# Output projection of a hybrid encoder layer: operands split inside the last branch block, first weights requested one block earlier, merged tiles fetched in eight steps

## The chip, the cores and the metric

The kernel runs on one core of a Trainium2 chip. The core has a matrix engine (TensorE, PE in the profile; PEld is its weight load), a vector engine (VectorE, DVE), a scalar engine (ScalarE, ACT), a general engine (GpSimd, POOL) and an engine that issues most DMA transfers (SyncE, SP). Each works through its own instructions in the order in which they stand; they wait for each other by semaphores. The metric is the time of one execution in device microseconds (us).

## The reference, cut to what matters

One encoder layer on x of 1024 rows and 2048 columns, in float32. The part that the change touches is the end:

```
y_a = windowed_gqa(q, k, v, ...) * silu(gate_a)
y_p = multiscale_pool(u, ...) * silu(gate_p)
g_a, g_p = split(sigmoid(h @ w_merge + b_merge))
merged = g_a * (y_a @ w_br_attn) + g_p * (y_p @ w_br_pool)
o = merged @ w_out                                    # 1024x2048 by 2048x2048
x + gate * rmsnorm(o, post_g)
```

So there are two branch products (1024 by 1024 by 2048 each), a gated sum called merged, one output product, and a norm over whole rows, which needs the squares of all 2048 columns of a row before any of that row can be written.

## The kernel before

**Numbers.** A float32 product is made of three matmuls: each operand is split into a high part in TensorE's fast float32 form (`hi`, a copy on ScalarE) and the rest (`lo`, a subtraction on VectorE); the product is hi by hi, lo by hi and hi by lo. `split` (line 94) makes the pair; its lines 95 (ScalarE) and 96 (VectorE) stand in the profile for every split.

**Fewer products.** Every large product is cut into two by two blocks and made by the Strassen-Winograd scheme: seven block products, not eight. `MOVING` names the seven moving operands in their order: B11, T3, T2, B21, T4, T1, B22; the weights that go with them are A11, S3, S2, A12, A22, S1, S4. The results build up in PSUM banks called X, V and Z, of two each, and are read out by VectorE and ScalarE; a bank can be written again only after it was read.

**Branch products.** `strassen` (line 210) does 256 output columns of a weight; the loop over `b` and `i` calls it eight times for each branch. `run` (line 321) steps through it; the last of the seven products of one call (B22, held in `late`) is run inside the next call, or by `flush`. Between the products `finish` (line 1065) multiplies a result by its gate and, for the second branch, adds the first branch's part, which comes from DRAM (`mp_d`). The gate is read from DRAM into a ring of four `gt` buffers, `fetch_gate`, and a new one is asked for when an old one has been used; ScalarE makes the sigmoid (line 1057). Merged columns 0 to 511 of the sequence stay in SBUF, in tiles `m` (`mt`, eight of them, two block rows by four `jp`); columns 512 to 1023 go to DRAM (`m_d`) through `pv`, for the second half. `merged_sums` makes the first sums (T1's and T2's operands) of one `jp`.

**Output product.** It is done in four blocks by `out_pair` (line 1163): halves 0 and 1 of the rows, and within each `i` = 0 and 1, two groups of columns. Here the merged values stand on TensorE as the weights, and the output weights are the moving side: in the profile `whi` and `wlo` are the split output weights, `mh` and `ml` the split merged operands. `put_op` (line 1098) makes operand n of one `jp`; both its splits and sums are pinned. One `out_pair` runs the seven products; each asks for four weight tiles (`wr`, 512 KB each, a ring of four), splits them into a ring of four `whi` and four `wlo`, and issues six matmuls for each of eight split weights (lines 1131 to 1133). After each quarter of a product a function is called that does what has to go between: `between_00` makes the next operand and, near its end, loads the other half's merged tiles from `m_d` (16 transfers of 256 KB); `between_01` makes sums and operands of the other half; `between_10` and `between_11` bring back rows of the first half (`mo` from `o_d`, and rows of x), finish them and store them. `pg` are the two rows of gains of a block. In the fourth block the last product's weights are all split ahead, the third block of rows is finished (`third_block`), and then the last two row tiles one by one.

**What sets the order.** A planner in the kernel framework orders the instructions of each engine by its estimates of when they can run, except those that `keep` pins to the program's order. The order is fixed when the kernel is built. TensorE, VectorE, ScalarE and SP then run their lists strictly in that order; a DMA that waits for a buffer or for an earlier store holds up every later DMA on SP.

Of the kernel before, what the change touches and what calls it, by code (L numbers as in the profile page):

```python
# [20 lines left out]
P = 128  # L21
# [21 lines left out]
def encoder_layer(ctx: ExitStack, tc: tile.TileContext, x, c, table, w_ada, b_ada, pre_g,  # L43
# [21 lines left out]
    def pool(name, bufs=1, **kw):  # L65
        return tc.tile_pool(name=name, bufs=bufs, reuse_waits="tile", **kw)
# [9 lines left out]
    def uid(s):  # L76
        cnt[0] += 1
        return f"{s}_{cnt[0]}"
# [4 lines left out]
    def slot(name, dt=F32R, shape=(P, 512)):  # L83
        return big.tile(list(shape), dt, tag="big", name=uid(name))
# [5 lines left out]
    def keep(ins):  # L90

        tc.keep_in_program_order(ins)
# [228 lines left out]
    def run(gen, side=None, every=(0, 2, 4, 6), at=()):  # L321
        for i in range(7):
            if i == 2:
                flush()
            else:
                next(gen)
                if fills:
                    fills.popleft()()
            for n, step in at:
                if n == i:  # L330
                    step()
            if side and i in every:
                side.popleft()()
        late.append(gen)
# [685 lines left out]
    ev_ctx.close()  # L1020
    ev_ctx = ExitStack()
    ev = ev_ctx.enter_context(pool("ev3", 6, side="right"))
    for b, w in enumerate((w_ba, w_bp)):
        op = new_op()
        fill_op(op, range(4), *ys[b], now=7 if b else 3)
        if b == 0:
            side.extend(y_steps(yp_d, ys[1]))
        else:
            ysrc.close()
            ev_ctx.close()  # L1030
            ev_ctx = ExitStack()
            ev = ctx.enter_context(pool("ev4", 4, side="right"))
            mr = ctx.enter_context(pool("mraw", side="right"))

            def merged_tiles():

                return [[mr.tile([P, 2, 512], F32, tag="m", name=uid("m"), bufs=2 * JP) for _ in range(JP)]
                        for _ in range(2)]

            def merged_sums(m, t2, jp):  # L1040

                b12 = m[0][jp][:, :, 256:512]
                keep(sub(b12, b12, m[0][jp][:, :, 0:256]))
                t2[jp] = mr.tile([P, 2, 256], F32, tag="t2", name=uid("t2"), bufs=JP)
                keep(sub(t2[jp], m[1][jp][:, :, 256:512], b12))

            mt, mt2 = merged_tiles(), {}
            side.extend([lambda: None] * 25)
            for jp in range(JP - 1):
                side[6 * jp + 7] = lambda jp=jp: merged_sums(mt, mt2, jp)  # L1050
        gates = {}

        def fetch_gate(i, blk, b=b):
            gt = ev.tile([P, 512], F32, tag="gt", name=uid("gt"), bufs=4)
            load(gt, block(proj_d, NIN + b * D + i * 256)(blk))
            col = 64 + b * KT + 2 * i + (1 if blk[0] == "2" else 0)
            nc.scalar.activation(gt, gt, AF.Sigmoid, bias=cols[:, col:col + 1])  # L1057
            gates[i, blk] = gt

        wanted = deque((i, blk) for i in range(8) for blk in ("11", "21", "22", "12"))  # L1060
        for _ in range(4):
            fetch_gate(*wanted.popleft())

        for i in range(8):
            def finish(blk, ps, addend, res, gates=gates, i=i, b=b):
                gt = gates.pop((i, blk))
                if ps is not None and addend is None:
                    nc.vector.tensor_tensor(res, ps, gt, ALU.mult)
                else:
                    if ps is not None:  # L1070
                        add(res, ps, addend)
                    nc.vector.tensor_tensor(res, res, gt, ALU.mult)
                if b == 0:
                    store(block(mp_d, i * 256)(blk), res)
                else:
                    if blk[1] == "1":
                        dst = mt[int(blk[0]) - 1][i // 2][:, i % 2]
                    else:
                        dst = ev.tile([P, 512], F32, tag="pv", name=uid("pv"), bufs=2)
                    load(dst, block(mp_d, i * 256)(blk))  # L1080
                    add(dst, dst, res)
                    if blk[1] == "2":
                        store(block(m_d, i * 256)(blk), dst)
                if wanted:
                    fetch_gate(*wanted.popleft())

            run(strassen(w, i * 256, rows_apart, range(4), op, ev, finish), side,
                () if b == 0 and i == 0 else (0, 2, 4) if b == 0 or i < 7 else (0, 1, 2, 3))
        flush()
        assert not side  # L1090

    merged_sums(mt, mt2, JP - 1)
    ssq = const.tile([P, NB, 4], F32, name="ssq_o")

    def put_op(n, jp, op, m, t2):


        name = MOVING[n]
        b11, b12, b21, b22 = (m[kh][jp][:, :, c * 256:(c + 1) * 256] for kh in range(2) for c in range(2))
        src = {"B11": b11, "T3": b11, "T2": t2[jp], "B21": b21, "T4": b21, "T1": b12, "B22": b22}[name]
        hi, lo = slot("mh", F32R, (P, 2, 256)), slot("ml", F32R, (P, 2, 256))
        split(hi, lo, src, True)
        op[name][jp] = hi, lo
        if name == "B11":
            keep(sub(b11, t2[jp], b11))
        elif name == "B21":
            keep(sub(b21, b21, t2[jp]))  # L1110

    def fetch_merged(m, kh):
        for jp in range(JP):
            for n in range(2):
                k = 2 * (2 * jp + n) + kh
                load(m[kh][jp][:, n], m_d[k * P:(k + 1) * P, 512:1024])

    def weights(name, i, jp):

# [39 lines left out]
    def row_tiles():  # L1159
        m = mr.tile([P, 2, 512], F32, tag="m", name=uid("mo"), bufs=2 * JP)  # L1160
        return m[:, 0], m[:, 1]

    def out_pair(half, i, op, between, after=None):


# [1 line left out]
        stays = half == 1 or i == 1  # L1167
        count = iter(range(7))
        g = {}
        for nh in range(2):  # L1170
            g[nh] = ev.tile([P, 512], F32, tag="ev", name=uid("pg"))
            n0 = nh * (D // 2) + i * 512
            load(g[nh], pg_d[0:1, n0:n0 + 512].to_broadcast([P, 512]))

        def split_weights(wname, ring=True):
            for jp in range(JP):
                raw = weights(wname, i, jp)
                for jj in range(2):
                    hi, lo = (wp.tile([P, 512], F32R, tag=t, name=uid(t), bufs=4) if ring else slot(t)
                              for t in ("whi", "wlo"))  # L1180
                    split(hi, lo, raw[:, jj])
                    yield hi, lo

        def product(wname, mov, pbs, fresh=False):

            ws = split_weights(wname)
            n, nj = next(count), 2 * JP
            for j in range(nj - 2):
                w = next(ws)
                for t in range(2):  # L1190
                    out_mm(pbs[t], op, mov, j, t, w, fresh and j == 0, False)
                if j % 2:
                    between(n, j // 2)
            w = list(ws)
            for t in range(2):
                for j in (nj - 2, nj - 1):
                    out_mm(pbs[t], op, mov, j, t, w[j - nj + 2], False, j == nj - 1)
            between(n, JP - 1)
# [21 lines left out]
        def kept(tag):  # L1220
# [3 lines left out]
        bx, bz, bv = ([bank(tag, b) for tag in tags] for b, tags in  # L1224
                      (("X", ("mm", "mm")), ("Z", SEEDED), ("V", ("sc", "sc"))))
        product("A11", "B11", bx, True)
        for t in range(2):
            nc.scalar.activation(bz[t], bx[t], AF.Copy)
        product("S3", "T3", bv, True)
# [9 lines left out]
            add(u2[t], bv[t], u2[t])  # L1239
            result("21", t, u2[t], u2[t])  # L1240
        product("S1", "T1", bz)
        ws = list(split_weights("S4", ring=False)) if final else None
        u4 = copies([slot("u4", F32) for _ in range(2)] if final else tiles("u4"), bz)
        for t in range(2):
            add(p7[t], p7[t], u4[t])
            result("22", t, p7[t], p7[t])
# [13 lines left out]
            for n in (0, 2, 3, 1):  # L1260
                finish_block(6 + t, n, scale)

    ops = [new_op(JP), new_op(JP)]
    for jp in range(JP):
        put_op(0, jp, ops[0], mt, mt2)
    nextm, nextt2 = [], {}
    scales = {}
    side = deque()
# [22 lines left out]
    def steps(n):  # L1291
        for _ in range(n):
            if side:
                side.popleft()()

    def between_00(n, jp):
        if n < 6:
            put_op(n + 1, jp, ops[0], mt, mt2)
        if jp == JP - 1 and n == 5:
            nextm.extend(merged_tiles())  # L1300
            fetch_merged(nextm, 0)
        if jp == JP - 1 and n == 6:
            fetch_merged(nextm, 1)

    def between_01(n, jp):

        if n == 1:
            merged_sums(nextm, nextt2, jp)
        for k in ((), (), (0,), (1, 2), (3,), (4,), (5,))[n]:
            put_op(k, jp, ops[1], nextm, nextt2)  # L1310
# [74 lines left out]
```

## Time and profile before

| | |
|---|---|
| median of 3 runs | 2163.8 us (2154.8 to 2165.83) |
| span of the profiled execution | 2152.0 us; the page gives no time around it |
| TensorE busy | 2098.7 us, 98% |
| VectorE, ScalarE busy | 1539.9 us (72%), 1129.6 us (52%) |
| mean granted TensorE clock | 0.996 |
| DMA | 466.11 MB, mean 217 GB/s |

The last branch product ends and the output product begins near 1820 us; the four output blocks take the rest. Times in a timeline are microseconds from the start of the span. A matmul's shown duration overlaps the next one's, so the pace is read from start to start. SPq is SP's queue: a row there is an issue, and the transfer lands some microseconds later.

### The profile page before, as it was taken

The numbers are of one execution on the slowest core, as the hardware profiler recorded it, in microseconds if no ns is written. First come the engines' busy times: TensorE is split into PE (matmuls) and PEld (weight loads), VectorE is DVE, ScalarE is ACT, GpSimd is POOL, SyncE is SP. The second block draws the span as 40 slices with busy tenths as digits, with TensorE's granted clock in tenths as the row PEclk, the third lists the DMA queues.
The fourth block names the chain that finished last, engine by engine and source line by source line (L and its number), as shares of the span: only waits on it lengthen the run. The fifth ranks groups of instructions, "written<-read, shape, count | busy, mean of one in ns | idle before, by whom it ended". The sixth has DMA issues, their size and how long they took to land.

```text
span 2152.0 us, 28951 instructions
## 1 busy us (share of the span) xinstructions
PE 2098.7 (98%) x9567; PEld 1716.3 (80%) x9567; DVE 1539.9 (72%) x2754; ACT 1129.6 (52%) x2124; POOL 7.4 (0%) x66
## 2 busy tenths in 40 slices
PE   6999999999999999999999999999999999999998
PEld 4588888887878888888888887888788887878886
DVE  5786666776547676777776878566967877879666
ACT  5654444443474546767765443334645544757654
POOL 0000000000000000000000000000000000000000
PEclk9999999999999999999999999999999999999999
DMA  9986566898666355545445765755654655686996
GB/s 333 290 277 202 188 203 212 296 316 271 227 224 206 118 175 199 171 158 186 161 150 189 220 223 192 238 177 177 229 175 156 230 167 175 207 287 215 303 314 226
DMA packets 303255, 466.11 MB, mean 217 GB/s; under 512 B 23882, under 2 KB 144866, under 8 KB 303104
## 3 DMA queue, kind: packets, MB, share of 16 engines
q1 hardware_dynamic: 301648, 462.02, 65.3%
q0 software_dynamic: 1120, 2.19, 0.3%
q8 instruction: 75, 1.23, 0.2%
q14 instruction: 76, 0.62, 0.1%
q10 hardware_dynamic: 336, 0.06, 0.0%
HBM read 340.41 MB, written 125.85 MB: 217 GB/s over the span
## 4 chain that ended last, share of the span: by engine, by line
PE 84%; DMA 8%; DVE 4%; ACT 2%; issue 1%; SPq 1%; DVEq 0%; ACTq 0%
PE Z L235 28%; PE X L235 18%; PE V L235 18%; DMA raw<-in_w_merge_dram 3%; PE Z L1131 2%; PE Z L1132 2%; PE Z L1133 2%; PE V L1131 1%; PE V L1133 1%; PE V L1132 1%; PE X L1132 1%; PE X L1133 1%; PE X L1131 1%; DVE wlo L96 1%; DMA xt<-in_x_dram 1%
## 5 line engine op out<-in xcount | busy, mean ns | idle before, releaser
L95 ACT ACTIVATE whi<-raw 128x512 fp32r<-128x512 f32 (+1 forms) x528 | 320.2, 610 | 509.1 <-PE Z L235 265.3
L96 DVE TENSOR_TENSOR wlo<-raw,whi 128x512 fp32r<-128x512 f32 (+1 forms) x528 | 346.9, 662 | 191.4 <-PE Z L235 114.6
L96 DVE TENSOR_TENSOR wlo<-wr,whi 128x512 fp32r<-128x512 f32 x224 | 150.9, 689 | 62.5 <-ACT whi L95 57.7
L95 ACT ACTIVATE whi<-wr 128x512 fp32r<-128x512 f32 x224 | 138.1, 628 | 99.6 <-DVE wlo L96 35.3
L102 DVE TENSOR_TENSOR raw<-raw,raw 128x512 f32<-128x512 f32 x80 | 55.2, 690 | 95.1 <-DMA raw<-in_w_merge_dram 73.2
L235 PE MATMUL V<-T3h,whi 128*128 128x512 f32 x336 | 92.3, 393 | 6.2 <-DVE u L102 6.2
L1057 ACT ACTIVATE gt<-gt,cols 128x512 f32<-128x512 f32 x64 | 46.0, 723 | 99.0 <-DMA gt<-proj_d 74.1
L235 PE MATMUL X<-B11h,whi 128*128 128x512 f32 x336 | 92.5, 393 | 3.2 <-DVE part L102 1.9
L235 PE MATMUL Z<-B22h,whi 128*128 128x512 f32 x336 | 92.8, 395 | 0.9 <-ACT u L290 0.9
L235 PE MATMUL Z<-T1h,whi 128*128 128x512 f32 x336 | 91.8, 392 | 0.9 <-ACT T1h L95 0.9
L235 PE MATMUL V<-T4h,whi 128*128 128x512 f32 x336 | 92.2, 392 | 0.0
L235 PE MATMUL X<-B11l,whi 128*128 128x512 f32 x336 | 92.1, 393 | 0.2 <-DVE B11l L96 0.2
L235 PE MATMUL X<-B11h,wlo 128*128 128x512 f32 x336 | 91.5, 392 | 0.0
L235 PE MATMUL Z<-T2h,whi 128*128 128x512 f32 x336 | 91.3, 391 | 0.0
L235 PE MATMUL Z<-T1l,whi 128*128 128x512 f32 x336 | 91.0, 390 | 0.1
L235 PE MATMUL Z<-B22l,whi 128*128 128x512 f32 x336 | 90.9, 390 | 0.0
L235 PE MATMUL X<-B21h,whi 128*128 128x512 f32 x336 | 90.9, 390 | 0.0
L235 PE MATMUL V<-T3l,whi 128*128 128x512 f32 x336 | 90.9, 390 | 0.0
L235 PE MATMUL V<-T4l,whi 128*128 128x512 f32 x336 | 90.8, 390 | 0.0
L235 PE MATMUL V<-T4h,wlo 128*128 128x512 f32 x336 | 90.8, 389 | 0.0
L235 PE MATMUL Z<-T1h,wlo 128*128 128x512 f32 x336 | 90.7, 390 | 0.0
L235 PE MATMUL Z<-T2l,whi 128*128 128x512 f32 x336 | 90.7, 390 | 0.0
(306 smaller groups left out, 4849.9 us busy)
## 6 DMA issues: line engine op xcount, KB each, us to landing
part<-part_d SPq DMA_DIRECT2D x136, 256.0 KB, 4.9
ada<-in_w_ada_dram SPq DMA_DIRECT2D x128, 256.0 KB, 4.7
raw<-in_w_in_dram SPq DMA_DIRECT2D x64, 512.0 KB, 4.0
raw<-in_w_merge_dram SPq DMA_DIRECT2D x64, 512.0 KB, 5.7
wr<-ws_dS SPq DMA_DIRECT2D x64, 512.0 KB, 5.4
wr<-in_w_out_dram SPq DMA_DIRECT2D x48, 512.0 KB, 5.2
proj_d<-part SPq DMA_DIRECT2D x68, 256.0 KB, 2.2
sw<-in_w_out_dram SPq DMA_DIRECT2D x64, 256.0 KB, 5.4
```

The costliest lines, as they stand in the source:

```text
L95: ins = (nc.scalar.activation(hi, src, AF.Copy), nc.vector.tensor_tensor(lo, src, f32(hi), ALU.subtract))
L96: nc.vector.tensor_tensor(lo, src, f32(hi), ALU.subtract))
L102: return (eng or nc.vector).tensor_tensor(o, a, b, ALU.add)
L235: nc.tensor.matmul(ps, w_[:, i], op[mov][j][m_], start=fresh and i == 0 and n == 0, stop=i == nj - 1 and n == 2, skip_group_check=True)
L1057: nc.scalar.activation(gt, gt, AF.Sigmoid, bias=cols[:, col:col + 1])
L1131: nc.tensor.matmul(pb, hi, w[0], start=first, stop=False, skip_group_check=True)
L1132: nc.tensor.matmul(pb, lo, w[0], start=False, stop=False, skip_group_check=True)
L1133: nc.tensor.matmul(pb, hi, w[1], start=False, stop=last, skip_group_check=True)
```

## The change

1. `put_op` and `ssq` move ahead of the branch loop. In the last call of the second branch (`b == 1 and i == 7`), `run` now does `put_op(0, jp, ...)` for `jp` 0 to 2 after the first, second and third step, and after the sixth step the last `merged_sums` and the last `put_op(0, ...)`. Before, all of these stood after the branch loop.
2. When a block's seventh product begins its last quarter, the four weight tiles of A11 of the next block are requested; `split_weights` uses them later. Before, they were requested when the next block began.
3. The gains `pg` are loaded after a block's first product, not at its start.
4. The second half's merged tiles are fetched in eight pieces of two transfers, over the sixth and seventh product of the first block and the first product of the second. Before: eight transfers after the sixth product and eight after the seventh.
5. In the fourth block six of the eight S4 weights are split, then come the copies of Z (`u4`), then the last two splits, which are pinned.

The amount of work is the same; no instruction is added or removed.

```diff
+            at = []
+            if b == 1 and i == 7:
+                at = [(1 + jp, lambda jp=jp: put_op(0, jp, ops[0], mt, mt2)) for jp in range(JP - 1)]
+                at += [(5, lambda: merged_sums(mt, mt2, JP - 1)), (5, lambda: put_op(0, JP - 1, ops[0], mt, mt2))]
             run(strassen(w, i * 256, rows_apart, range(4), op, ev, finish), side,
-                () if b == 0 and i == 0 else (0, 2, 4) if b == 0 or i < 7 else (0, 1, 2, 3))
+                () if b == 0 and i == 0 else (0, 2, 4) if b == 0 or i < 7 else (0, 1, 2, 3), at)
...
-    merged_sums(mt, mt2, JP - 1)
...
-    def fetch_merged(m, kh):
-        for jp in range(JP):
-            for n in range(2):
-                k = 2 * (2 * jp + n) + kh
-                load(m[kh][jp][:, n], m_d[k * P:(k + 1) * P, 512:1024])
+    def fetch_merged(m, kh, jp):
+        for n in range(2):
+            k = 2 * (2 * jp + n) + kh
+            load(m[kh][jp][:, n], m_d[k * P:(k + 1) * P, 512:1024])
...
+    first_raws = []
...
-        def split_weights(wname, ring=True):
+        def split_weights(wname, ring=True, pin=()):
             for jp in range(JP):
-                raw = weights(wname, i, jp)
+                raw = first_raws.pop(0) if wname == "A11" and first_raws else weights(wname, i, jp)
...
-                    split(hi, lo, raw[:, jj])
+                    split(hi, lo, raw[:, jj], 2 * jp + jj in pin)
...
             w = list(ws)
+            if n == 6:
+                first_raws.extend(weights("A11", 1 - i, jp) for jp in range(JP))
...
         product("A11", "B11", bx, True)
+        fetch_gain()
...
-        ws = list(split_weights("S4", ring=False)) if final else None
+        if final:
+            last = split_weights("S4", ring=False, pin=(6, 7))
+            ws = [next(last) for _ in range(6)]
         u4 = copies([slot("u4", F32) for _ in range(2)] if final else tiles("u4"), bz)
+        if final:
+            ws += list(last)
...
-    for jp in range(JP):
-        put_op(0, jp, ops[0], mt, mt2)
...
+    later = deque((kh, jp) for kh in range(2) for jp in range(JP))
+
+    def fetch_next():
+        if later:
+            fetch_merged(nextm, *later.popleft())
+
     def between_00(n, jp):
         if n < 6:
             put_op(n + 1, jp, ops[0], mt, mt2)
-        if jp == JP - 1 and n == 5:
+        if n == 4 and jp == JP - 1:
             nextm.extend(merged_tiles())
-            fetch_merged(nextm, 0)
-        if jp == JP - 1 and n == 6:
-            fetch_merged(nextm, 1)
+        if n >= 5 and jp:
+            fetch_next()
...
     def between_01(n, jp):
 
+        if n == 0 and jp:
+            fetch_next()
```

More of the change, by code (lines that the diff above doesn't have):

```diff
@@ L1022, in encoder_layer, with put_op @@
     ev = ev_ctx.enter_context(pool("ev3", 6, side="right"))
+    ssq = const.tile([P, NB, 4], F32, name="ssq_o")
+    def put_op(n, jp, op, m, t2):
+        name = MOVING[n]
+        b11, b12, b21, b22 = (m[kh][jp][:, :, c * 256:(c + 1) * 256] for kh in range(2) for c in range(2))
+        src = {"B11": b11, "T3": b11, "T2": t2[jp], "B21": b21, "T4": b21, "T1": b12, "B22": b22}[name]
+        hi, lo = slot("mh", F32R, (P, 2, 256)), slot("ml", F32R, (P, 2, 256))
+        split(hi, lo, src, True)
+        op[name][jp] = hi, lo
+        if name == "B11":
+            keep(sub(b11, t2[jp], b11))
+        elif name == "B21":
+            keep(sub(b21, b21, t2[jp]))
+    ops = [new_op(JP), new_op(JP)]
     for b, w in enumerate((w_ba, w_bp)):
@@ L1085, in finish @@
                     fetch_gate(*wanted.popleft())
+            at = []
+            if b == 1 and i == 7:
+                at = [(1 + jp, lambda jp=jp: put_op(0, jp, ops[0], mt, mt2)) for jp in range(JP - 1)]
+                at += [(5, lambda: merged_sums(mt, mt2, JP - 1)), (5, lambda: put_op(0, JP - 1, ops[0], mt, mt2))]
             run(strassen(w, i * 256, rows_apart, range(4), op, ev, finish), side,
-                () if b == 0 and i == 0 else (0, 2, 4) if b == 0 or i < 7 else (0, 1, 2, 3))
+                () if b == 0 and i == 0 else (0, 2, 4) if b == 0 or i < 7 else (0, 1, 2, 3), at)
         flush()
         assert not side
-    merged_sums(mt, mt2, JP - 1)
[L1096 to L1110, printed above, removed]
-    def fetch_merged(m, kh):
-        for jp in range(JP):
-            for n in range(2):
-                k = 2 * (2 * jp + n) + kh
-                load(m[kh][jp][:, n], m_d[k * P:(k + 1) * P, 512:1024])
+    def fetch_merged(m, kh, jp):
+        for n in range(2):
+            k = 2 * (2 * jp + n) + kh
+            load(m[kh][jp][:, n], m_d[k * P:(k + 1) * P, 512:1024])
     def weights(name, i, jp):
@@ L1169, in out_pair, with fetch_gain @@
         g = {}
[L1170 to L1173, printed above, removed]
-        def split_weights(wname, ring=True):
+        def fetch_gain():
+            for nh in range(2):
+                g[nh] = ev.tile([P, 512], F32, tag="ev", name=uid("pg"))
+                n0 = nh * (D // 2) + i * 512
+                load(g[nh], pg_d[0:1, n0:n0 + 512].to_broadcast([P, 512]))
+        def split_weights(wname, ring=True, pin=()):
             for jp in range(JP):
-                raw = weights(wname, i, jp)
+                raw = first_raws.pop(0) if wname == "A11" and first_raws else weights(wname, i, jp)
                 for jj in range(2):
@@ L1261, in out_pair @@
                 finish_block(6 + t, n, scale)
-    ops = [new_op(JP), new_op(JP)]
-    for jp in range(JP):
-        put_op(0, jp, ops[0], mt, mt2)
     nextm, nextt2 = [], {}
```

## The prediction

> **What bounds the kernel now.** I read the page first, then the list of what TensorE waited for, then the timelines of TensorE, ScalarE, VectorE and the DMA queue around each wait, then the chain of waits. The page gives the span and TensorE's share; the waits are those of the last 652 us, where the output projection (lines 1131 to 1133) lies.
>
> ```profile
> span 2152.0 us, 28951 instructions
> PE 2098.7 (98%) x9567; PEld 1716.3 (80%) x9567; DVE 1539.9 (72%) x2754; ACT 1129.6 (52%) x2124; POOL 7.4 (0%) x66
> PE X L1132 <- DVE ml L96: 3.9, 1, 3.9
> PE X L1131 <- ACT whi L95: 2.9, 1, 2.9
> PE Z L1131 <- ACT u L1206: 2.2, 1, 2.2
> PE V L1131 <- ACT whi L95: 0.8, 1, 0.8
> ```
>
> TensorE is busy 98% of the span, and the change removes no matmul, so it can only win idle time. In the output projection there are four idle places, 9.8 us together. The first has a slow tail (a row of a timeline: start, duration, engine, line, out<-in, idle time before and its releaser):
>
> ```profile
> 1817.56 1.07 PE L235 MATMUL Z<-T1h,whi 128*128 128x512 f32 x4
> 1820.28 0.61 PE L1131 MATMUL X<-whi,mh 128*128 128x512 f32 x2
> 1821.12 1.19 PE L235 MATMUL Z<-B22h,whi 128*128 128x512 f32 x4 [0.23 <-ACT u L290]
> 1828.06 0.80 PE L1132 MATMUL X<-whi,ml 128*128 128x512 f32 x1 [3.92 <-DVE ml L96]
> 1828.65 0.63 PE L1133 MATMUL X<-wlo,mh 128*128 128x512 f32 x1
> 1833.35 0.49 PE L1133 MATMUL X<-wlo,mh 128*128 128x512 f32 x1
> 1833.67 0.39 PE L1131 MATMUL X<-whi,mh 128*128 128x512 f32 x1
> ```
>
> From 1817.56 to 1820.28 twelve matmuls take 2.72, a step of 0.227. From 1820.28 to 1833.67 there are 27 of them (2, then 12 of the last branch product, then 13 singles whose first two and last are shown): 6.1 at that step, 13.4 in fact. **The first place costs 7.3**: some 4.7 of waiting, and after 1828.65 eleven steps of 0.43 (4.70 to 1833.35), that is a slowed clock, for 2.6 with the restart. The others are read below.
>
> **Place 1, operands made in the last branch pair.** `put_op(0, ...)` for three tiles now comes inside the last `strassen`, pinned in program order; TensorE's order hardly changes (two more X matmuls ahead of the last branch product). On VectorE and ScalarE the moved work now stands ahead of things that release others:
>
> ```profile
> 1810.96 0.72 ACT L1057 ACTIVATE gt<-gt,cols 128x512 f32<-128x512 f32 x1 [2.78 <-DMA gt<-proj_d]
> 1813.63 0.62 ACT L95 ACTIVATE mh<-m 128x512 fp32r<-128x512 f32 x1
> 1814.15 0.58 ACT L245 ACTIVATE u<-Z 128x512 f32<-128x512 f32 x1
> 1816.46 0.72 ACT L1057 ACTIVATE gt<-gt,cols 128x512 f32<-128x512 f32 x1 [1.73 <-DMA gt<-proj_d]
> 1812.85 0.68 DVE L1068 TENSOR_TENSOR c<-Z,gt 128x512 f32<-128x512 f32 x1
> 1815.25 0.69 DVE L1068 TENSOR_TENSOR c<-X,gt 128x512 f32<-128x512 f32 x1
> 1818.95 0.68 DVE L102 TENSOR_TENSOR u<-V,u 128x512 f32<-128x512 f32 x1
> 1827.32 0.69 DVE L96 TENSOR_TENSOR ml<-m,mh 128x512 fp32r<-128x512 f32 x1
> 1828.04 0.69 DVE L105 TENSOR_TENSOR m<-t,m 128x512 f32<-128x512 f32 x1
> 1813.56 0.32 SPq L1055 DMA_DIRECT2D gt<-proj_d  x1
> ```
>
> Steps read here: ScalarE 0.52 (0.63 after a gate), VectorE 0.60, or 0.72 where it needs the result just made. In the order that the changed kernel is built with, the first mh starts at 1812.6 (a split and a copy after the gate of 1810.96, ahead of two weight splits), so its ml at 1813.24 and `m<-t,m` at 1813.96 go ahead of `c<-Z,gt`, which moves from 1812.85 to 1814.57. Its end frees the buffer of the last gate: that load moves from 1813.56 to 1815.28, and the sigmoid, which came 2.90 behind the load, from 1816.46 to 1818.18. Behind this sigmoid on ScalarE stand two mh (1818.81, 1819.33) and the first two out weights (to 1820.98). VectorE waits for those mh in order: ml 1819.45, ml, two m differences, and only then `c<-X,gt` at 1821.85, which ran at 1815.25 before. That read frees the bank of the first output tile: TensorE, ready at 1820.28, starts at 1822.56, **2.28** late. Its third matmul waits for wlo (1822.45 to 1823.14): **0.15**. The fourth needs the bank of V, freed by `u<-V,u` at 1823.65 to 1824.34 (1818.95 before): **0.98**. On ScalarE the fourth mh needs the finished tile (`m<-m,c` ends 1823.74); then a weight split; then `u<-Z` at 1824.8 to 1825.4, for which the last branch product waits: **0.84**. It ends at 1828.3, twelve more X matmuls at 1830.9; the next wlo stands thirteen steps of 0.60 behind VectorE's 1824.25, one of them 0.72, at 1832.2 to 1832.9: **2.05**. Together 6.3, with four restarts of 0.11 (from 2132.23 to 2132.57, shown under place 4, is 0.34) 6.7.
>
> Is the clock kept? The lowest price is nothing, the highest the 2.6 just seen. The row nearest to after's idle pieces (2.28 at most, but three within 5 us) is elsewhere in the kernel:
>
> ```profile
> 1330.67 1.19 PE L235 MATMUL X<-B11h,whi 128*128 128x512 f32 x4 [1.85 <-DVE part L102]
> 1331.70 1.83 PE L235 MATMUL X<-B11l,whi 128*128 128x512 f32 x4
> 1333.32 1.91 PE L235 MATMUL X<-B11h,wlo 128*128 128x512 f32 x4
> ```
>
> There 1.85 of idle was followed by two groups of four that took 1.83 and 1.91 instead of 1.07, 1.6 more in all, while the idle 2.93 and 2.20 shown below were followed by none. One in three: I take 0.5. So 7.2 for place 1 after the change against 7.3: **no gain**, between 0.6 gained and 2.0 lost (6.7 to 9.3).
>
> [...]
>
> On SP the first pair's gains (`pg`) now wait for a buffer of the ending branch, with the stores of the last merged rows behind. The second quarter of the second product's weights goes out some 8 us later (about 1833.5); with a landing of 5 to 7 (6.5 and 7.3 below) they come at 1839 to 1841, and are wanted when that product's first quarter is done, about 1842. I cost it at nothing; without that cover it is 2 to 3. No work of POOL's queue is moved or passed.
>
> **Place 2, weights ahead and merged tiles spread (first to second pair).**
>
> ```profile
> 1906.62 0.39 PE L1133 MATMUL Z<-wlo,mh 128*128 128x512 f32 x1
> 1909.93 0.50 PE L1131 MATMUL X<-whi,mh 128*128 128x512 f32 x1 [2.93 <-ACT whi L95]
> 1902.59 6.58 DMA wr<-in_w_out_dram
> 1911.24 0.37 SPq L1122 DMA_DIRECT2D wr<-ws_dS  x1
> DMA to landing us min/median/max: 7.3/7.3/7.3
> 1896.00:1920.00 24.00, 20.96 (x89) 16.11 (x88) 12.93 (x21) 11.69 (x24) 0.00 (x0) 1.00 0.93 303
> ```
>
> The second pair's first A11 weights are issued at 1902.59 and land 6.58 later: TensorE starts 3.31 behind the matmul before, 3.1 lost, some 3.5 with the restarts. The change puts their load ahead of ten transfers of 256 KB (two stores of p, six merged loads, two `pg`); at the 303 GB/s of the last row that is 8.7 of queue, so it is in place and this wait goes. What is late next is the S3 weights: issued at 1911.24, landed 7.3 later at 1918.5. With the wait gone A11 starts at 1906.85, its 48 matmuls take 10.9, and S3 wants its first weights about 0.7 before 1917.7. The transfers ahead are the same (16 merged, 8 stores, 2 `pg`, 12 weights), and the last row (DMA share 0.93) leaves little room to land sooner. With the landing unmoved S3 waits 1.9 with its restart; if the weights' own order closes all gaps, nothing; if `pg` and merged loads pile up, 2.6. I take 1.1, between the two nearer: **gain 2.4** (0.9 to 3.5).
>
> **Place 3, third to fourth pair.**
>
> ```profile
> 2059.85 7.01 DMA out_dram<-mo
> 2067.77 6.48 DMA wr<-ws_dS
> 2075.04 0.50 PE L1131 MATMUL V<-whi,mh 128*128 128x512 f32 x1 [0.78 <-ACT whi L95]
> ```
>
> A load of an old row into `mo` waits at the head of SP for a 7.0 store; the S3 weights behind it go out at 2067.77, land 6.48 later, and S3 waits 0.8, some 1.3 with the issue and restarts. Now the first S3 load stands ahead of the last such row, but the other three stay behind it, and A11's four loads ahead of the stores lengthen these. The 1.3 goes; late next is the second S3 load, between nothing and 2.8. I take 1.0: **gain 0.3** (1.3 to -1.5).
>
> **Place 4, copies ahead of two splits.**
>
> ```profile
> 2129.64 0.39 PE L1133 MATMUL Z<-wlo,mh 128*128 128x512 f32 x1
> 2132.23 0.50 PE L1131 MATMUL Z<-whi,mh 128*128 128x512 f32 x1 [2.20 <-ACT u L1206]
> 2132.57 0.40 PE L1132 MATMUL Z<-whi,ml 128*128 128x512 f32 x1
> 2130.54 1.15 ACT L95 ACTIVATE whi<-wr 128x512 fp32r<-128x512 f32 x2 [1.01 <-DMA wr<-ws_dS]
> 2131.60 1.07 ACT L1206 ACTIVATE u<-Z 128x512 f32<-128x512 f32 x2
> ```
>
> The copies stand behind two splits whose weights land at 2130.5. Ahead of them, they follow the product, and 2.2 of the 2.5 (2.36 and a restart) go. The seventh weights are then wanted 18 steps, 4.1, after about 2130; split at 2130.5 to 2132, they cover. The stores of rows 4 and 5 move behind the p sums on VectorE, at 0 to 0.6 of the tail; I take 0.3. **Gain 1.9** (1.6 to 2.2).
>
> **Sum.** 0.1 + 2.4 + 0.3 + 1.9 = 4.7, span about 2147.3; ends 7.6 gained and 1.0 lost. The page shows only the span; the lowest of the three runs is 2.8 above it and the median 11.8, so the profiled execution stands near the lowest, and what varies between the runs is larger than the gain. On the median I put 2163.8 - 4.7 = **2159**.
>
> **Rivals.** *All four waits go, as the new places of the work suggest*: 7.3 + 3.5 + 1.3 + 2.2 = 14.3, 2149.5. For it: each moved step is one that a wait named. Against: the order of VectorE and ScalarE walked above, and the busy DMA. *The loads ahead clog the queue (slower)*: SP issues in order, a store took 7.0 to land, and in the second, third and fourth pair four A11 loads now go before stores for which `mo` loads wait at SP's head. Each S3 load kept back by one more store costs its 7.0 less the 2 to 3 that the split ring covers, 4 to 5; from one such case on it is slower: place 2 and 3 both hit, and no other gain but place 4's, 2 x 4.5 - 1.9 = 7 slower, 2171; with three it passes the bound. Against: only the 0.8 of place 3 is of that kind today, and the second to third pair shows no wait at all. *The moved work was hidden anyway*: only place 4 counts, 2162.
>
> **How the numbers follow.** Forecast (places 2 and 4, place 1 unchanged) 0.60, own range 2156 to 2165; all waits go 0.13; clogged queue 0.17, half of it past the bound; hidden anyway 0.10. About 0.5%, 10.8, is what a measurement tells from no change: faster 0.13, same 0.78, slower 0.09. Low end 2149 from the first rival, which is also near the lowest of the three less the sum (2150); high end 2168, the forecast's upper end and half of the clogged queue.
>
> **What would show it.** Right: TensorE waits at the first output product for VectorE `c` and `u`, and for `u L290`, in pieces of 2.3 and 1.0, and a 2 us wait for wlo soon after; no wait at A11 of the second pair, a shorter one at its S3; `u L1206` waits under 0.5. Wrong: no wait at the first product (faster), waits of 4 or more for weights behind SP (slower), or slow matmuls behind the first product beyond 1.5.

## The result, and the profile after

The changed kernel takes 2151.8 us (median of 10 runs, 2144.4 to 2154.4) beside 2161.3 of the kernel before in its 10 runs. The ratio is 0.9960, with a 95% interval of 0.9948 to 0.9972. A second timing on another occasion gave 0.9972 (0.9961 to 0.9984). So it is faster by 6 to 9 us, less than the half per cent that the prediction set as its bound, and 1.3 to 1.8 times the 4.7 us forecast.

The page of the changed kernel, and its list of what TensorE waited for from 1800 us on (what waited, for what; us in total, times, longest):

```profile
span 2149.9 us, 28954 instructions
PE 2100.2 (98%) x9567; PEld 1717.1 (80%) x9567; DVE 1537.6 (72%) x2754; ACT 1129.0 (53%) x2124; POOL 7.4 (0%) x66
```

```profile
PE X L1134 <- DVE c L1085: 2.3, 1, 2.3
PE V L1134 <- ACT whi L95: 1.3, 1, 1.3
PE X L1134 <- DVE u L102: 0.7, 1, 0.7
PE Z L235 <- ACT u L290: 0.6, 1, 0.6
```

The page counts three instructions more than before; the counts of PE, DVE, ACT and POOL are the same. The four waits of before (`ml` 3.9, `whi` 2.9 and 0.8, `u` 2.2) are replaced by these. Three of the four are the ones forecast for the first output product, and the other is the S3 wait of the second pair.

Place 1, in the timeline of TensorE, then VectorE and ScalarE (start, duration, engine, line, operation, idle time before and its releaser):

```profile
1822.45 1.07 PE L235 MATMUL Z<-T1h,wlo 128*128 128x512 f32 x4
1825.81 0.47 PE L1134 MATMUL X<-whi,mh 128*128 128x512 f32 x1 [2.29 <-DVE c L1085]
1826.35 0.47 PE L1136 MATMUL X<-wlo,mh 128*128 128x512 f32 x1
1827.52 0.50 PE L1134 MATMUL X<-whi,mh 128*128 128x512 f32 x1 [0.70 <-DVE u L102]
1828.59 2.08 PE L235 MATMUL Z<-B22h,whi 128*128 128x512 f32 x4 [0.56 <-ACT u L290]
1830.46 1.91 PE L235 MATMUL Z<-B22l,whi 128*128 128x512 f32 x4
1832.17 1.91 PE L235 MATMUL Z<-B22h,wlo 128*128 128x512 f32 x4
1834.73 0.41 PE L1134 MATMUL X<-whi,mh 128*128 128x512 f32 x1
```

```profile
1823.78 1.29 DVE L105 TENSOR_TENSOR m<-t,m 128x512 f32<-128x512 f32 x2
1824.98 0.68 DVE L1085 TENSOR_TENSOR c<-X,gt 128x512 f32<-128x512 f32 x1
1826.78 0.68 DVE L102 TENSOR_TENSOR u<-V,u 128x512 f32<-128x512 f32 x1
```

```profile
1821.29 0.72 ACT L1074 ACTIVATE gt<-gt,cols 128x512 f32<-128x512 f32 x1 [3.53 <-DMA gt<-proj_d]
1827.95 0.58 ACT L290 ACTIVATE u<-Z 128x512 f32<-128x512 f32 x1
```

TensorE would have gone on at 1823.36 (four matmuls of 0.227 after 1822.45). It starts 2.45 late, because the bank of X is read by `c<-X,gt` only at 1824.98, behind the `m<-t,m` of two moved operands. The matmul for the next bank comes 0.94 late, for `u<-V,u`; the last branch product 0.84 late, for the copy `u<-Z`. Then the groups of four take 1.9 to 2.1 instead of 1.07: fourteen steps of up to 0.6, 3.0 lost, until 1834.73 (a step is the time from the start of one matmul to that of the next). The granted clock is 0.50 from 1828.5 to 1834.7, and 0.99 behind it; before, it was 0.50 from 1828.0 to 1833.5, and 1.00 behind that. Together 7.3, as much as before.

Places 2 and 4 (TensorE, then ScalarE at place 4):

```profile
1909.74 0.39 PE L1134 MATMUL X<-whi,mh 128*128 128x512 f32 x1
1920.39 0.39 PE L1136 MATMUL X<-wlo,mh 128*128 128x512 f32 x1
1922.07 0.50 PE L1134 MATMUL V<-whi,mh 128*128 128x512 f32 x1 [1.29 <-ACT whi L95]
2129.59 0.39 PE L1136 MATMUL Z<-wlo,mh 128*128 128x512 f32 x1
2129.82 0.45 PE L1134 MATMUL Z<-whi,mh 128*128 128x512 f32 x1
```

```profile
2129.14 0.58 ACT L1216 ACTIVATE u<-Z 128x512 f32<-128x512 f32 x1
2130.02 0.60 ACT L1216 ACTIVATE u<-Z 128x512 f32<-128x512 f32 x1 [0.29 <-PE Z L1136]
2130.61 0.63 ACT L95 ACTIVATE whi<-wr 128x512 fp32r<-128x512 f32 x1
```

A11 of the second pair starts with no wait, its S3 waits 1.29, some 1.8 with the restarts. At place 4 there is no idle time of TensorE: the copies of Z come at once, and the last two splits behind them.

**A measure for all runs.** The part ahead of the output product has the same order of instructions in all kernels here up to the last branch pair, yet the start of its last T1 product lies between 1815.3 and 1827.8 us in twelve profiles. So totals of single profiles say little, and I compare stretches behind that point instead. A stretch is cut at the first matmul of A12 of a block, and what it lost is its length less its number of matmuls at 0.2267. Stretch 1 runs from the last T1 product of the branches to A12 of the first block (168 matmuls): before, 1862.91 less 1817.56 is 45.35, less 38.08 is 7.27. Stretch 2 runs on to A12 of the second block, stretch 3 from A12 of the third to that of the fourth, stretch 4 from there to the last matmul; what lies between 2 and 3 loses 0.1 to 0.2 in all twelve. They are a little wider than the prediction's places. Each row is one profiled execution:

| lost, us | stretch 1 | 2 | 3 | 4 |
|---|---|---|---|---|
| before | 7.3 | 4.2 | 1.5 | 2.5 |
| before, second profile | 6.4 | 5.1 | 1.3 | 6.9 |
| operands moved only | 6.9 | 4.5 | 3.1 | 6.7 |
| copies ahead only | 6.2 | 4.9 | 2.8 | 0.6 |
| weights ahead only | 6.4 | 1.6 | 0.2 | 2.7 |
| merged tiles spread only | 7.4 | 8.1 | 2.3 | 4.4 |
| all but the operands | 6.3 | 2.2 | 1.2 | 0.6 |
| all but the operands, idle time filled | 4.7 | 2.6 | 1.2 | 0.0 |
| after | 7.3 | 2.0 | 0.5 | 0.1 |
| after, second profile | 6.6 | 2.3 | 0.7 | 1.1 |
| after, fewer operands, later | 1.6 | 1.8 | 2.5 | 0.2 |
| the same, merged tiles sooner | 0.5 | 4.7 | 0.3 | 0.1 |

### The profile page after: what moved, and what is told of

Read it like the earlier page. It is cut to its first block, busy times and chain, and to the rows that moved or that the text cites. A ratio compares the mean times of both kernels' runs of the same rounds, so it can differ in the third digit from the quotient of the medians.

```text
span 2149.9 us, 28954 instructions
## 1 busy us (share of the span) xinstructions
PE 2100.2 (98%) x9567; PEld 1717.1 (80%) x9567; DVE 1537.6 (72%) x2754; ACT 1129.0 (53%) x2124; POOL 7.4 (0%) x66
## 4 chain that ended last, share of the span: by engine, by line
PE 85%; DMA 6%; DVE 5%; ACT 1%; issue 1%; SPq 0%; ACTq 0%; DVEq 0%; POOLq 0%
PE Z L235 29%; PE V L235 19%; PE X L235 19%; PE Z L1134 2%; PE Z L1135 2%; PE Z L1136 2%; PE V L1136 1%; PE V L1134 1%; PE V L1135 1%; PE GEMV L453 1%; DMA raw<-in_w_merge_dram 1%; DVE wlo L96 1%; PE X L1136 1%; PE X L1135 1%; PE X L1134 1%
## 5 line engine op out<-in xcount | busy, mean ns | idle before, releaser
L235 PE MATMUL Z<-B22h,wlo 128*128 128x512 f32 x336 | 91.4, 392 | 0.0
L235 PE MATMUL Z<-T2h,wlo 128*128 128x512 f32 x336 | 90.8, 390 | 0.0
```

The costliest lines, as they stand in the source:

```text
L235: nc.tensor.matmul(ps, w_[:, i], op[mov][j][m_], start=fresh and i == 0 and n == 0, stop=i == nj - 1 and n == 2, skip_group_check=True)
```

## The experiments

My theory after the result: places 1 to 4 went as forecast in the two profiles, some 5 in all (15.5 less 9.9 in the table), and the other 3 to 4 us of the medians lie in what varies from run to run. The rival: moving the operands wins after all, and the profile of before or after hid it.

### The kernel before, again

> The kernel before, unchanged, so its ratio is 1.000 within its interval. What is asked is how a second profile of it divides: theory A, that the part ahead of the output product varies from execution to execution by some 3 us, expects a section ahead of 1820 us that comes out 2 to 4 longer than in the first profile, with the four places of the output section again near 7.3, 3.6, 1.3 and 2.5. Theory B, that the first profile caught an output section with few waits, expects the same section ahead and places that cost 3 to 5 more together.

Measured: ratio 1.0001 (0.9987 to 1.0015). Theory A fell in its sign: the part ahead was 2.3 shorter in this profile, not longer. Theory B held for the stretches, though the section ahead was not the same: they cost 19.7 instead of 15.5, and stretch 4 alone costs 4.4 more. TensorE there, and ScalarE:

```profile
2127.20 0.39 PE L1133 MATMUL Z<-wlo,mh 128*128 128x512 f32 x1
2131.32 0.80 PE L1131 MATMUL Z<-whi,mh 128*128 128x512 f32 x1 [3.73 <-ACT u L1206]
2131.91 0.63 PE L1132 MATMUL Z<-whi,ml 128*128 128x512 f32 x1
2137.03 0.57 PE L1132 MATMUL Z<-whi,ml 128*128 128x512 f32 x1
2137.43 0.40 PE L1133 MATMUL Z<-wlo,mh 128*128 128x512 f32 x1
```

```profile
2129.63 1.15 ACT L95 ACTIVATE whi<-wr 128x512 fp32r<-128x512 f32 x2 [1.56 <-DMA wr<-ws_dS]
2130.69 1.06 ACT L1206 ACTIVATE u<-Z 128x512 f32<-128x512 f32 x2
```

The first profile had shown a wait of 2.20 and no slow matmul here. In this one the last two S4 splits begin 2.4 after the last matmul of T1 instead of 0.9, since their weights landed that much later against it; the copies behind them come later too, TensorE idles 3.73, and its next thirteen matmuls run at a step of 0.43. Place 4 is worth 2.5 in one execution and 6.9 in another.

### Only the operands

```diff
+                at = [(1 + jp, lambda jp=jp: put_op(0, jp, ops[0], mt, mt2)) for jp in range(JP - 1)]
+                at += [(5, lambda: merged_sums(mt, mt2, JP - 1)), (5, lambda: put_op(0, JP - 1, ops[0], mt, mt2))]
```

> Only the operands of the first output product are moved into the last branch pair. Theory (the waits change their name, not their sum): 0, between 1 faster and 2 slower than before; TensorE waits for c, u and u of L290 at the first product, some 4.2 in three pieces, and a slow stretch of about 3. Rival (the move wins, which would also account for the 4 us that the medians gained beyond the traces): 4 to 7 faster, ratio 0.997 to 0.998.

Measured: ratio 1.0000 (0.9986 to 1.0014). The waits at the first product are those of the changed kernel (`c` 2.3, `u` 0.6, `u` of L290 0.3), stretch 1 costs 6.9. This part wins nothing; the rival, at 4 to 7, is outside the interval. Stretch 4 of this profile shows the long form again, 6.7.

### All but the operands

The change with the two lines above left out, and the operands made behind the branch loop as before.

> The whole change without the operands in the last branch pair. Theory: as fast as the changed kernel or up to 1 faster or slower, that is about 0.996 of before; place 1 has its old waits again (whi 2.9 and ml 3.9) at 7.3, places 2 to 4 cost 1.8, 0.3 and 0.1. Rival (the move wins): 4 to 7 slower than the changed kernel, ratio 0.998 to 0.999.

Measured: ratio 0.9962 (0.9948 to 0.9977), that of the whole change. Stretch 1 has its old `ml` wait and costs 6.3. From both sides, then: the first part of the change is worth nothing that the runs show; its own interval allows 3 us either way.

### Only the copies

```diff
+        if final:
+            last = split_weights("S4", ring=False, pin=(6, 7))
+            ws = [next(last) for _ in range(6)]
         u4 = copies([slot("u4", F32) for _ in range(2)] if final else tiles("u4"), bz)
+        if final:
+            ws += list(last)
```

> Only the copies of Z go ahead of the last two S4 splits. Theory: the wait for u at the last product goes, 2.2 to 2.4 gained, the tail 0.3 longer, so 2 faster than before, ratio 0.9990 (within 0.9986 to 0.9995). Rival (something else then ends late, the S4 weights first of all): a wait for whi of 1 to 2 takes its place, less than 1 gained, ratio 0.9995 to 1.000.

Measured: ratio 0.9976 (0.9967 to 0.9986), 5 us, where the theory said 2 and the rival less than 1. Both missed on the same side. Stretch 4 costs 0.6. This is the step that the prediction sized too low. Five profiles without it give 2.5, 2.7, 4.4, 6.7 and 6.9, a mean of 4.6; seven with it give 0.0 to 1.1, a mean of 0.4. The difference, 4.2, agrees with the timed 5.

### Only the weights ahead, and only the spread

The first takes parts 2 and 3 of the change alone, the second part 4 alone.

> Only the first weights of each block are requested ahead and the gains come after the first product; the merged tiles stay in two lumps. Theory (the transfers in front of those weights made the wait at A11, and the S3 weights are late next): no wait at A11 of the second pair, 1.5 to 2.6 at its S3 instead, place 3 within 1 of before; 1 to 3 faster, ratio 0.9986 to 0.9995. Rival (the eight steps of the merged tiles are what frees the queue): S3 waits 3 or more, ratio 0.9995 to 1.0005.

> Only the merged tiles are fetched in eight steps. Theory (the queue is as full as before, the wait only moves): the wait at A11 of the second pair falls from 3.1 to 1 to 2, and a later quarter of A11 waits 1.5 to 4 behind the merged loads that now stand there; ratio 0.9992 to 1.0010. Rival (the spread alone empties the queue): both waits under 1.5 together, 2 faster, ratio about 0.999.

Measured: weights ahead 0.9982 (0.9967 to 0.9997); spread 1.0006 (0.9989 to 1.0023). With the weights ahead there is no wait at A11, S3 of the second pair waits 0.8, and stretches 2 and 3 cost 1.6 and 0.2. The theory holds in its kind; the wait at S3 is shorter than the 1.5 to 2.6 that it gave, and 3.9 us faster is above its 1 to 3, with an interval too wide to tell. With the spread alone A11 waits 1.2 at its start and then 3.07 for its last quarter. The third line is what SP waited for from 1905 to 1918, the fourth the issue of that quarter's weights:

```profile
1919.84 0.39 PE L1132 MATMUL X<-wlo,mh 128*128 128x512 f32 x1
1923.30 0.79 PE L1130 MATMUL X<-whi,mh 128*128 128x512 f32 x1 [3.07 <-ACT whi L95]
SPq L1217 <- DVE u L1213: 6.3, 2, 5.4
1916.09 0.39 SPq L1124 DMA_DIRECT2D wr<-in_w_out_dram  x1
```

The weights stand behind two merged transfers and, more important, behind two stores of `u` that hold SP: VectorE makes `u` behind the splits of A11, which are late themselves, so the first wait breeds the second. Stretch 2 costs 8.1 instead of 4.2 to 5.1 in this one profile: the wait was moved and grew. The time resolves neither a loss nor a gain. What wins at place 2 is part 2 with part 3, not the eight steps of the merged tiles.

### Fewer operands, later

```diff
-                at = [(1 + jp, lambda jp=jp: put_op(0, jp, ops[0], mt, mt2)) for jp in range(JP - 1)]
-                at += [(5, lambda: merged_sums(mt, mt2, JP - 1)), (5, lambda: put_op(0, JP - 1, ops[0], mt, mt2))]
+                at = [(3, lambda: put_op(0, 0, ops[0], mt, mt2)), (5, lambda: put_op(0, 1, ops[0], mt, mt2))]
...
         flush()
         assert not side
+        if b:
+            put_op(0, 2, ops[0], mt, mt2)
+            merged_sums(mt, mt2, JP - 1)
+            put_op(0, 3, ops[0], mt, mt2)
```

> The changed kernel, but with fewer operands moved and later: jp 0 after the fourth step of the last branch pair, jp 1 after the sixth, jp 2 and 3 behind the branch loop. Theory (place 1 gains nothing in the change because the moved work stands ahead of c, u and u of L290): these three run where they ran before the change, TensorE waits only in pieces of 0.2 to 0.8 for wlo, 1.5 to 2.5 together, with no slow stretch; place 1 costs 2 to 3 instead of 7.3, and the kernel is 4 to 6 faster than the changed one, ratio 0.993 to 0.994. Rival (place 1 costs what it does because the amount of work for VectorE and ScalarE between the last branch results and the first product is too large, wherever it stands): the waits move to wlo and ml of the first product and stay above 5; ratio 0.995 to 0.997.

Measured: ratio 0.9947 (0.9933 to 0.9962), median 2150.3. TensorE and VectorE at place 1:

```profile
1829.61 1.07 PE L235 MATMUL Z<-T1h,wlo 128*128 128x512 f32 x4
1830.51 0.39 PE L1137 MATMUL X<-whi,mh 128*128 128x512 f32 x1
1831.65 1.09 PE L235 MATMUL Z<-B22h,whi 128*128 128x512 f32 x4
1841.02 0.50 PE L1139 MATMUL X<-wlo,mh 128*128 128x512 f32 x1 [0.15 <-DVE wlo L96]
```

```profile
1826.14 0.69 DVE L105 TENSOR_TENSOR m<-t,m 128x512 f32<-128x512 f32 x1
1826.75 0.69 DVE L1085 TENSOR_TENSOR c<-X,gt 128x512 f32<-128x512 f32 x1
1829.68 0.68 DVE L102 TENSOR_TENSOR u<-V,u 128x512 f32<-128x512 f32 x1
```

With one operand ahead of it and not three, `c<-X,gt` runs 3.8 before TensorE wants the bank; the output product starts without a gap and no matmul is slow. Stretch 1 costs 1.6 instead of 6.6 to 7.3. That is the theory's mechanism: the order on VectorE, not the amount of work, cost place 1. The ratio is above the 0.993 to 0.994 expected. The 4 to 6 us that it gave are not all in the total, since stretch 3 of this profile lost 2.5 where the changed kernel lost 0.5 and 0.7. In the profiles' four stretches it is 4 us better than the changed kernel (6.0 beside 9.9 and 10.6, unrounded); the ratio is lower than the changed kernel's two, 0.9960 and 0.9972, but the intervals overlap. It beats the kernel before; that it beats the changed one is likely and not settled.

### The idle time filled

All but the operands, with 16 matmuls into a bank that nobody reads, in the 4.1 us before the first `ml`. The matmuls of the last branch product are pinned too (not shown), so that the 16 come behind them:

```diff
+    spare, mh0 = bank("at", "spare"), ops[0]["B11"][0][0]
+    for _ in range(16):
+        keep(nc.tensor.matmul(spare, mh0[:, 0, 0:P], mh0.rearrange("p a b -> p (a b)"), start=True, stop=True,
+                              skip_group_check=True))
```

> All but the operands, as before, plus 16 matmuls into a spare bank in the 4.1 us in which TensorE waits for ml at the first output product; their result is not used. Theory (the slow matmuls behind that wait come from the idle time ahead of them): the 16 take about 3.7 at 0.23 a step, the wait after them is under 0.6, and no step of 0.43 follows, where 6 to 11 did (1.2 to 2.2 lost); place 1 costs 4.1 to 4.6. Rival (the slowed clock has another cause, such as load, or time since the last slowing): six or more steps of 0.43 in the 16 or behind them, and place 1 stays at 5.5 to 7.3.

Measured, first without and then with them:

```profile
1830.78 1.07 PE L235 MATMUL Z<-B22h,wlo 128*128 128x512 f32 x4
1835.76 0.80 PE L1131 MATMUL X<-whi,ml 128*128 128x512 f32 x1 [3.91 <-DVE ml L96]
1836.35 0.63 PE L1132 MATMUL X<-wlo,mh 128*128 128x512 f32 x1
1838.49 0.63 PE L1132 MATMUL X<-wlo,mh 128*128 128x512 f32 x1
```

```profile
1828.25 1.07 PE L235 MATMUL Z<-B22h,wlo 128*128 128x512 f32 x4
1829.16 3.79 PE L1283 MATMUL spare<-mh 128*128 128x512 f32 x16
1833.24 0.50 PE L1137 MATMUL X<-whi,ml 128*128 128x512 f32 x1 [0.29 <-DVE ml L96]
1833.57 0.39 PE L1138 MATMUL X<-wlo,mh 128*128 128x512 f32 x1
1833.80 0.40 PE L1137 MATMUL X<-whi,ml 128*128 128x512 f32 x1
```

The data come no sooner, but the step behind the wait is 0.23 instead of 0.43; stretch 1 costs 4.7 instead of 6.3. So the slow matmuls came from the idle time ahead of them here. The six profiles with this wait as it was before (3.9 idle, not filled) all show five to eleven steps of about 0.43 behind it; this one, the only one with it filled, shows none. The granted clock is 0.50 from 1835.7 to 1838.5 without the 16, and 1.00 from 1829 to 1838 with them. The timed ratio, 0.9953 (0.9936 to 0.9969) beside 0.9962, does not resolve 1.6 us.

### The changed kernel, again, and the merged tiles sooner

> The changed kernel, unchanged: ratio 0.996, within 0.9945 to 0.9975. What is asked is how a second profile of it divides. Theory (the waits that the change takes away are the ones that vary): from the start of the last T1 product of the branches to the last matmul 319 to 321, as in the first profile (319.9), the last product of the fourth block waits under 0.6, and the part ahead of it differs by some us without any difference in the order. Rival (the changed kernel varies there as the kernel before does, 325.5 and 329.7): 323 or more.

Measured: ratio 0.9972 (0.9961 to 0.9984), at the edge of what was expected. From the last T1 product to the last matmul it takes 320.6, as the theory said (319.9 the first time); the kernel before took 325.5 and 329.7. The last product waited 0.8 for `u`, a little more than the 0.6 expected: in this execution the fifth and sixth split, behind which the copies still stand, came late themselves.

The other kernel is that of "fewer operands, later" with the merged tiles asked for in each quarter of the sixth and seventh product and none in the next block:

```diff
-        if n >= 5 and jp:
+        if n >= 5:
             fetch_next()
...
-        if n == 0 and jp:
-            fetch_next()
```

> The kernel with fewer operands, moved later (316.0 from the start of the last T1 product of the branches to the last matmul), with the eight pieces of merged tiles fetched over the sixth and seventh product alone, so that none stands ahead of the S3 weights of the second pair. Theory (the DMA engines are full from 1875 on, at 0.93 to 1.03, so the order of the queue changes little): S3 of the second pair still waits 0.8 to 2, within 1.5 of that kernel, ratio 0.9935 to 0.996. Rival (the three late pieces are what keeps the S3 weights back): no wait there, 1.5 to 2 faster, the section 314; its opposite, that the pieces now delay the A11 weights or S4's: a new wait of 1 to 3 at A11 of the second pair or at S4.

Measured: ratio 0.9958 (0.9943 to 0.9974).

```profile
PE V L1137 <- ACT whi L95: 2.2, 1, 2.2
PE Z L1137 <- ACT u L1219: 1.5, 1, 1.5
```

The DMA engines of the changed kernel were full there (the columns after PEclk are their mean share and GB/s):

```profile
1875.00:1890.00 15.00, 15.00 (x68) 12.43 (x67) 12.94 (x21) 11.37 (x25) 0.00 (x0) 1.00 0.93 321
1910.00:1920.00 10.00, 10.00 (x46) 8.29 (x45) 4.51 (x7) 3.48 (x7) 0.00 (x0) 1.00 1.03 335
```

S3 of the second pair waits 2.2, not less; and a new wait of 1.5 comes before S4 of the first block, where one copy `u<-Z` stands behind two splits whose weights now land late: place 4's pattern in another block. The rival fell. In this profile the three late pieces are not what keeps the S3 weights back, and asking for them sooner only moves the loss forward (stretch 2: 4.7 instead of 1.8).

## Why the prediction was right or wrong

**Place 1 (0.1 gained, between 0.6 gained and 2.0 lost): right in its three waits, and in its size by luck, since two of its terms were wrong and cancelled.** The three pieces came as walked through: 2.45 and a restart of 0.08, 0.94 and 0.84, beside 2.28, 0.98 and 0.84. The 0.15 for the first wlo did not come. The clock's 0.5 was 3.0, beyond the 1.5 that the prediction had named as a sign of being wrong, and the 2.05 for the later wlo did not appear: TensorE, at half its pace, asked for it some 3 later than forecast. The gains on SP cost nothing, as put: the first block's S3 does not wait. Over all profiles stretch 1 costs 6.7 with the old place of the operands (six) and 6.9 with the new one (three), and the timed ratio of that part alone is 1.0000.

The slow steps came behind a shorter idle time than before: the longest of after's place 1 is 2.29, where 3.92 stood ahead of those of before. In the counts of the last section the same gap went either way; why gaps of 2.0 to 3.2 were followed by slow steps about half the time, no run here shows.

**Place 2 (2.4): right.** Stretch 2 costs 4.7 in four profiles without the weights ahead (the spread alone, 8.1, left out), and 2.2 in five with parts 2 to 4 and the merged tiles as in the change: 2.5 gained. The wait at A11 went and the one at S3 came, at 1.8 with restarts where 1.1 was put.

**Place 3 (0.3): sized low.** 2.2 in four profiles against 1.2 in five, a gain of 1.0; it varies between 0.5 and 2.5 in the changed order and between 1.3 and 3.1 in the old, so this is rough.

**Place 4 (1.9): the step that failed, by its size.** "2.2 of the 2.5 go" took one execution's wait for the place's cost. The mechanism stands: the copies stood behind two splits whose weights were late, and they now go ahead. But the last weights land 0.8 to 2.4 behind the start of T1's last matmul in the twelve profiles, and in the two old-order ones where that is 2.4 the wait is 3.7, and the slow steps follow. In the second profile of after, where it is 2.3, the wait is 0.8, above the 0.5 that the prediction allowed. Five profiles put the old cost at 2.5 to 6.9; the gain is 4.2, timed 5.

**The tail (0.3)** is 0.4 and 0.5: the time from the last matmul to the end of the span is 8.9 and 8.9 before, 9.3 and 9.4 after.

**The sum.** With -0.3, 2.5, 1.0, 4.2 and -0.4 the stretches give 7.0, where the forecast had 0.1, 2.4, 0.3, 2.2 and -0.3. That lies between the two timed results (0.0040 and 0.0028 of 2161 and 2159, 8.6 and 6.0). The predicted time was further off, 2159 against 2151.8: the 4.7 was taken from a median of three runs, 2163.8, which ten runs put at 2161.3, 2.5 of the 7.2. The 2151.8 lies below the forecast's own 2156 to 2165; the low end of 2149, which it is above, came from a rival that did not come true. Taken alone, the parts gave ratios of 1.0000 (part 1), 0.9982 (2 and 3), 1.0006 (4) and 0.9976 (5), which add up to 0.9964, between the two of the whole.

**The rivals.** "All four waits go" would have been 2149.5, not far from the time, but for another reason: place 1 kept its cost, and place 4 gave twice its price. "The loads ahead clog the queue" did not come in the changed kernel; the spread alone shows something of the kind (3.07, for weights behind stores that held SP). "The moved work was hidden anyway" is wrong for places 2 and 4.

The record carries place 4 one step further back. In all twelve profiles the first load of the fourth block's S4 weights goes out 12.0 before the start of T1's last matmul, the third 1.9 after the first has landed, and the fourth 1.8 after the third. The first takes 4.4 to 6.0 to land, and that is the spread that the last one inherits. What stays open: why that load takes up to 1.6 longer in some executions, and what makes stretch 3 vary by 2 us in kernels that are alike there.

## What to carry to other kernels

Price a wait that ends with a DMA from several profiles, not one: take the spread of the landing, and look whether the idle time at its long end is one behind which the matmuls ran slowly (here 23 of 42 gaps of 2.0 to 3.2, and 15 of 16 longer ones). When work is moved ahead to fill idle time, list what stands behind it on each engine; here, with one moved operand ahead of the read of a PSUM bank, stretch 1 cost 1.6 and 0.5, and with three it cost 6.9, as much as with the wait that they removed (6.7). A copy that frees a bank should not stand behind splits that wait for a load, in any block: here TensorE waited 2.20 and 3.73 for such a copy in the fourth, and 1.5 in the first.

## What the hardware showed that was not expected

TensorE's clock was slowed more behind an idle time of 2.29 than I had allowed for (after's place 1: 3.0 lost at a granted 0.50, where I put 0.5), and behind others as long it was not. In the twelve profiles, from 400 us on, I took every gap from start to start of two matmuls, less one step, of over 0.9, and counted those with four or more steps of about 0.43 within the next 10 us. Of 45 gaps under 1.5 three had them, each with a longer gap within 6 us; of 24 gaps of 1.5 to 2.0 none; of 42 gaps of 2.0 to 3.2, 23; of 16 longer ones, 15, among them all ten above 3.65. Of the 42, 38 stand alone, with no other gap over 0.45 within 8 us before or 6 us behind, and 19 of these had them. A fall mostly lasted six to thirteen steps, so it cost 1.2 to 2.6. The same wait in the same code fell on one side in one execution and on the other in the next: the wait ahead of a T3 product at 504 us was 3.46 without a slow step in the first profile of before, and 3.59 with eight in the second. Filling the gap took the slow steps away (none, where the six profiles that left it idle had five to eleven); only the one place was tried.
